# A mixture of experts whose outputs are added to a table in memory instead of being scattered by matmuls

## The chip, the core and the metric

The kernel runs on one core of one Trainium2 chip. The metric is the device time of one execution in microseconds. TensorE is called PE in the profile, VectorE DVE, ScalarE ACT, GpSimd POOL and SyncE SP; PEld is the weight load of a matmul. A trace is one profiled execution, with times in us from the start of its span.

## The reference

Two transformer blocks on 512 tokens of 1024 features. The first has differential attention, then a mixture of experts: 16 experts in 4 groups of 4; a token takes the likeliest group and in it the best two experts. The second block has forgetting attention with pooling, a convolution module and two convolutional feed-forward layers. The change lies in the mixture:

```
gates = one_hot(group) * (g_w * e_w)                     # (512, 16), two per token are not 0
hid = silu(t @ w_gate[e]) * (t @ w_up[e])                # 1024 -> 512, for each expert e
hid = hid * gates[:, e]
y = sum over e of hid @ w_down[e]                        # 512 -> 1024
x = x + g2 * y
```

All data are float32, and all 16 experts' weights (6 MB each) are read.

## The kernel before

The kernel multiplies in a split form: each float32 operand is taken as a high part (float32r, written by ACT) and a low part (the rest, by DVE), and `mm3` (lines 204 to 207) does three matmuls: high by high, high by low, low by high.

Weights come through the class `Weights`. A unit is a load of 1 MB into a raw buffer, issued by SP on the hardware queue; it is split in two halves of 128x1024 (line 106 on ACT for the high part, line 115 on DVE for the low part). In the mixture of experts there are four raw buffers and seven pairs of split buffers (lines 1010 and 1011); up to four units are loaded and six halves split ahead of the matmul that takes them. A raw buffer is free again, and SP issues the next load into it, when both its halves are split.

Features and experts. `moe_constants` (line 834, called near the end of attention) writes the shift of the second modulation, the same for all tokens, into the table `rows` in memory; later the scaled activations of all tokens, `h2tok`, are added to that table by four accumulating DMAs (line 1149). The router then gives each token its place among the tokens of an expert. An expert has 128 slots; `slots` (line 1209) turns them into row numbers (`idi`, and `idf` as a float), where an empty slot has number 600, out of bounds. `gather` (line 1227) clears a buffer on POOL and fetches an expert's rows by an indirect DMA; a row out of bounds is not fetched. Code for experts with more than 128 tokens stands behind a branch (lines 1297 to 1356).

The loop over the 16 experts (line 1453). Iteration e runs on PE in this order:

- `gate_up(e)`: 48 matmuls into two banks; ACT applies Silu, DVE multiplies with the gate and the up part into `sg`
- `x_tiles(e+1)`: eight transposes of the next expert's rows (line 1374), split by ACT and DVE into Xh and Xl
- `prep(e+2)`: four small matmuls that find the rows of the expert after that, and its gather
- `down(e-1)`: 24 matmuls into two banks; `down_evac(e-1)` splits them into Yh and Yl, and DVE writes a one-hot matrix S of slots by tokens (line 1436)
- `hid_t(e)`: four transposes of `sg`, split into Hh and Hl

Experts form groups of 3, 3, 3, 3 and 4 (line 1366). When a group's outputs are there, `scatter` (line 1438) brings them back to the tokens: for each of 8 blocks of 128 features, two matmuls per expert (Yh and Yl against S, lines 1444 and 1445, 512 columns each) add up in a `tp` bank, and DVE adds the bank, times the modulation, to the residual `xT` (line 1446). Four groups are handed out piecewise within the loop, one block per two halves of weights (`take`, line 1380); what is left is done at once two experts later. The last group of four runs after the loop, and each block is followed by `even_prep` (line 1501): the residual is stored, and the next layer's input is written as high (ACT) and low part (DVE).

The layout before: partition p of a weight tile holds rows k*128+p, so a load takes runs of one row: 2 KB for gate and up (512 columns), 4 KB for down (1024 columns).

Of the kernel before, what the change touches and what calls it, by code (L numbers as in the profile page):

```python
# [25 lines left out]
D = 1024  # L26
# [135 lines left out]
def kernel(ctx, tc, a, out):  # L162
# [657 lines left out]
    NONE = 600.0  # L820
    rows = dram.tile([S, D], FT, name="rows")
    gm2 = mk(mcp, (128, KT), FT, "gm2")
    wrg = mk(mcp, (128, KT, 20), FT, "wrg")
# [10 lines left out]
    def moe_constants():  # L834
# [19 lines left out]
        for x in range(2):  # L854
            V.tensor_scalar(first[:, x, :], iota_s[:, 0:4], -3.0 + 2.0 * x, None, op0=OP.add)
        for b in range(2):
            ps = bank("tp")
            for k in range(4):
                T.transpose(ps[:, k * 128:(k + 1) * 128], mod[:, SH2, 4 * b + k:4 * b + k + 1].to_broadcast([128, 128]),
                            ident)  # L860
            sh = mk(at, (128, S), FT, "t", 6)
# [152 lines left out]
    def moe_unit(w, k0, nk, n):  # L1014
        u = k_unit(w, k0, nk, 0, n, (raw_rings, split_rings, cnt[0], cnt[1]))
        cnt[0] += 1
        cnt[1] += 2
        return u
# [190 lines left out]
    def slots(oh, p, bufs=2, n=4):  # L1209
# [7 lines left out]
        V.tensor_scalar(idf, idf, NONE, None, op0=OP.add)  # L1217
        idi = mk(p, (128, 1), I32, "idi", bufs)
        V.tensor_copy(idi, idf)
# [18 lines left out]
    def prep(e, n=52):  # L1238
        idf, idi, i_ps = slots(OH[e], mp, n=n)
        xr = mk(mp, (128, D), FT, "xr", 2)  # L1240
        gather(idi, xr)
        ROWS[e] = (xr, idf)
        if n == 52:
            GC[e] = gate_of(e, mp, i_ps)

    mark(0)
    prep(0, 4)
# [49 lines left out]
    with tc.If(most > 128):  # L1297
        with tc.For_i(0, NE, 1) as ev:
            have = nc.values_load(count[0:1, ds(ev, 1)], min_val=0, max_val=S)
            with tc.If(have > 128):  # L1300
# [5 lines left out]
                for b in range(1, NT):  # L1306
                    idf, idi, i_ps = slots(one_hot(ov, pcol_e[:, :, None], 128 * b, 1), ov, 1, 52)
                    xr = mk(ov, (128, D), FT, "oxr")
                    gather(idi, xr)
                    gall = mk(ov, (128, NE), FT, "ogs")  # L1310
# [11 lines left out]
                    for name, ps in (("expert_w_gate", pg), ("expert_w_up", pu)):  # L1322
                        for q in range(2):
                            w = mk(ov, (128, 4, EF), FT, "ow", 3)
                            nc.sync.dma_start(w, a[name][0, ds(ev, 1), q * 512:(q + 1) * 512, :].rearrange(
                                "o (k p) n -> p (o k) n", p=128))
                            for k in range(4):
# [37 lines left out]
    A.activation(cmax, eps1, AF.Silu)  # L1365
    GROUPS = [(0, 3), (3, 6), (6, 9), (9, 12), (12, 16)]
    def x_tiles(e):
# [9 lines left out]

    spread_out, halves_taken = [iter(())], [0]

    def take(j):  # L1380

        halves_taken[0] += 1
        if halves_taken[0] % 2 == 0:
            next(spread_out[0], None)
        return ws.take(j)

    def gate_up(e):
        hi, lo, gc = XT.pop(e)
        banks = []
        for name in ("g", "u"):  # L1390
            ps = bank("mm")
            banks.append(ps)
            for q in range(2):
                for half in range(2):
                    w = take(U[name, e][q] + half)
                    for kk in range(2):
                        k = 4 * q + 2 * half + kk
                        mm3(ps, (hi[:, k, :], lo[:, k, :]), (w[0][:, kk, :], w[1][:, kk, :]), k == 0, k == KT - 1)
            if name == "g":
                sg = mk(mb, (128, EF), FT, "sg", 2)  # L1400
                A.activation(sg, ps, AF.Silu)
                if e + 2 < NE:
                    mark(e + 2)
        V.scalar_tensor_tensor(sg, sg, gc, banks[1], op0=OP.mult, op1=OP.mult)
        HID[e] = sg

    def hid_t(e):
# [4 lines left out]
        for k in range(4):  # L1412
            T.transpose(ps[:, k * 128:(k + 1) * 128], sg[:, k * 128:(k + 1) * 128], ident)
        split(ps.rearrange("p (a n) -> p a n", n=128), hi, lo)
        HT[e] = (hi, lo)

    def down(e):
        hi, lo = HT.pop(e)
        banks = [bank("sc"), bank("sc")]
        for k in range(4):  # L1420
            w = take(U["d", e][k // 2] + k % 2)
            for half in range(2):
                c = slice(half * 512, (half + 1) * 512)
                mm3(banks[half], (hi[:, k, :], lo[:, k, :]), (w[0][:, 0, c], w[1][:, 0, c]), k == 0, k == 3)
        DB[e] = banks

    def down_evac(e):
        banks = DB.pop(e)
        yh = mk(ysp, (128, D), FR, "Yh", 4)
        yl = mk(ysp, (128, D), FR, "Yl", 4)  # L1430
# [4 lines left out]
        ST[e] = mk(ysp, (128, S), FR, "S", 4)  # L1435
        V.tensor_scalar(ST[e], iota_s, ROWS.pop(e)[1], None, op0=OP.is_equal)

    def scatter(e0, e1, done=None):
        for m in range(KT):
            yield  # L1440
            ps = bank("tp")
            c = slice(m * 128, (m + 1) * 128)
            for e in range(e0, e1):
                T.matmul(ps, lhsT=Y[e][0][:, c], rhs=ST[e], start=e == e0, stop=False)  # L1444
                T.matmul(ps, lhsT=Y[e][1][:, c], rhs=ST[e], start=False, stop=e == e1 - 1)  # L1445
            V.scalar_tensor_tensor(xT[m], ps, mod[:, G2, m:m + 1], xT[m], op0=OP.mult, op1=OP.add)
            if done is not None:
                done(m)

# [3 lines left out]
    for e in range(NE):  # L1453
        if e in [e1 + 2 for _, e1 in GROUPS]:
            for _ in spread_out[0]:
                pass
        gate_up(e)
# [49 lines left out]
    ws.flush(len(ws.halves))  # L1507
    for _ in scatter(*GROUPS[-1], done=even_prep):
        pass
    lows.pop(0)()  # L1510
# [968 lines left out]
```

## Time and profile before

| | us |
|---|---|
| median of 3 runs | 1922.92 |
| lowest, highest | 1920.22, 1924.81 |
| profiled execution | 1918.79 |
| its span | 1917.0 |
| PE busy | 1860.0 |
| DVE busy | 1388.0 |
| ACT busy | 955.0 |

The mean granted clock of PE is 0.982 of full speed. A busy share is an average over stages; the stage in question lies between about 365 and 726 us. A matmul's row shows its full length with its pipeline, about 0.4 us for 512 columns, while the next one starts 0.23 us later: counts of matmuls are therefore priced by distances of starts, not by the length of a row. In the chain of waits a piece is what the end of the execution waited for at that time.

### The profile page before, as it was taken

How to read it: one execution, taken by the hardware profiler on the slowest of the kernel's cores; microseconds unless marked ns; L12 is line 12 of the kernel's file. 1: busy time of each engine (PE TensorE's matmuls, PEld its weight loads, DVE VectorE, ACT ScalarE, POOL GpSimd, SP SyncE). 2: the span in 40 equal slices, each digit the busy share in tenths (PEclk: the TensorE clock that was granted, in tenths of full speed). 3: DMA queues.
4: the chain of work that ended last, by engine and by line, in shares of the span. 5: the costliest groups of instructions: out<-in, count | busy, mean ns of one | idle time of the engine just before them, and what ended most of it. 6: DMA issues, size and time to landing. Idle time of an engine off the chain costs nothing.

```text
span 1917.0 us, 24466 instructions
## 1 busy us (share of the span) xinstructions
PE 1860.0 (97%) x9422; PEld 1524.7 (80%) x9423; DVE 1388.0 (72%) x2431; ACT 955.0 (50%) x1530; POOL 101.9 (5%) x144
## 2 busy tenths in 40 slices
PE   6999999699999999999999999999999999999999
PEld 5787766487888878877888888888778888898898
DVE  6888875699999988677676466367997766647752
ACT  4555554576776665555344244247574644324421
POOL 5000001110100001000000000000000000000000
PEclk9999989799999999999999999999999999999999
DMA  9644326698988872202232232223121222223232
GB/s 284 201 127 137 111 78 211 179 330 305 313 296 283 280 257 78 67 26 85 89 109 88 89 109 88 88 89 88 53 58 45 67 88 88 98 79 110 88 100 78
DMA packets 195947, 260.49 MB, mean 136 GB/s; under 512 B 7489, under 2 KB 144922, under 8 KB 195826
## 3 DMA queue, kind: packets, MB, share of 16 engines
q1 hardware_dynamic: 185378, 228.67, 36.3%
q0 software_dynamic: 10448, 30.20, 5.5%
q8 instruction: 76, 1.25, 0.3%
q14 instruction: 45, 0.37, 0.1%
HBM read 252.56 MB, written 10.49 MB: 137 GB/s over the span
## 4 chain that ended last, share of the span: by engine, by line
PE 86%; DVE 6%; DMA 4%; ACT 2%; issue 1%; SPq 0%; POOL 0%; POOLq 0%; ACTq 0%; DVEq 0%
PE mm L205 11%; PE mm L207 11%; PE mm L206 11%; PE sc L205 10%; PE sc L207 10%; PE sc L206 10%; PE tp L205 1%; PE tp L1444 1%; PE tp L206 1%; PE tp L207 1%; DVE lo L115 1%; PE tp L1445 1%; PE sc L719 1%; DMA ada_q<-in_ada_w_dram 1%; PE sc L2437 1%
## 5 line engine op out<-in xcount | busy, mean ns | idle before, releaser
L106 ACT ACTIVATE hi<-raw 128x1024 fp32r<-128x1024 f32 (+1 forms) x409 | 414.8, 1040 | 205.4 <-PE sc L2439 39.9
L115 DVE TENSOR_TENSOR lo<-raw,hi 128x1024 fp32r<-128x1024 f32 (+1 forms) x409 | 481.7, 1202 | 23.6 <-ACT hi L106 22.1
L205 PE MATMUL mm<-h,hi 128*128 128x512 f32 x592 | 242.3, 409 | 2.7 <-DVE vl L153 1.9
L206 PE MATMUL mm<-h,hi 128*128 128x512 f32 x592 | 234.6, 396 | 1.3 <-DVE h L153 1.3
L207 PE MATMUL mm<-h,lo 128*128 128x512 f32 x592 | 234.7, 396 | 0.0
L205 PE MATMUL sc<-h,hi 128*128 128x512 f32 x552 | 219.4, 397 | 0.0
L207 PE MATMUL sc<-h,lo 128*128 128x512 f32 x552 | 217.8, 395 | 0.2 <-DVE lo L115 0.2
L206 PE MATMUL sc<-h,hi 128*128 128x512 f32 x552 | 217.2, 394 | 0.0
L2045 ACT ACTIVATE y<-u,VC 128x512 f32<-128x512 f32 x88 | 71.7, 817 | 161.2 <-DVE u L153 161.1
L205 PEld LDWEIGHTS mm<-h,hi 128*128 128x128 f32 x592 | 112.6, 190 | 30.9 <-issue 7.0
L153 DVE SCALAR_TENSOR_TENSOR y<-u,VC,y 128x511 f32<-128x511 f32 (+1 forms) x176 | 131.5, 748 | 3.4 <-ACT y L2045 0.2
L207 PEld LDWEIGHTS mm<-h,lo 128*128 128x128 f32 x592 | 112.2, 190 | 25.7
L206 PEld LDWEIGHTS mm<-h,hi 128*128 128x128 f32 x592 | 112.7, 190 | 24.6 <-DVE h L153 2.4
L207 PEld LDWEIGHTS sc<-h,lo 128*128 128x128 f32 x552 | 104.0, 188 | 24.7 <-DVE lo L115 0.9
L205 PEld LDWEIGHTS sc<-h,hi 128*128 128x128 f32 x552 | 104.2, 189 | 23.4 <-issue 0.9
L206 PEld LDWEIGHTS sc<-h,hi 128*128 128x128 f32 x552 | 104.2, 189 | 23.0
L205 PE MATMUL mm<-hi,Xh 128*128 128x512 f32 x256 | 103.4, 404 | 0.0
L206 PE MATMUL mm<-lo,Xh 128*128 128x512 f32 x256 | 102.1, 399 | 0.0
L207 PE MATMUL mm<-hi,Xl 128*128 128x512 f32 x256 | 102.0, 398 | 0.0
L153 DVE TENSOR_TENSOR u<-sc,rb 128x512 f32<-128x512 f32 x51 | 35.2, 691 | 85.1 <-PE sc L207 81.3
L153 DVE TENSOR_TENSOR u<-mm,rb 128x512 f32<-128x512 f32 x37 | 25.5, 691 | 66.7 <-PE mm L207 62.8
L2055 ACT ACTIVATE act<-y 128x512 fp32r<-128x512 f32 x44 | 27.8, 632 | 82.6 <-DVE y L153 82.6
(567 smaller groups left out, 3991.7 us busy)
## 6 DMA issues: line engine op xcount, KB each, us to landing
raw<-in_ffn_w_up_dram SPq DMA_DIRECT2D x44, 1024.0 KB, 5.1
raw<-in_expert_w_gate_dram SPq DMA_DIRECT2D x32, 1024.0 KB, 6.9
raw<-in_expert_w_up_dram SPq DMA_DIRECT2D x32, 1024.0 KB, 7.6
raw<-in_expert_w_down_dram SPq DMA_DIRECT2D x32, 1024.0 KB, 7.1
ada_w<-in_ada_w_dram POOLq DMA_DIRECT2D x32, 512.0 KB, 4.0
raw<-in_ffn_w_down_dram SPq DMA_DIRECT2D x16, 1024.0 KB, 5.2
ada_q<-in_ada_w_dram SPq DMA_DIRECT2D x32, 256.0 KB, 6.8
raw<-in_odd_w_pw_dram SPq DMA_DIRECT2D x16, 512.0 KB, 4.2
```

The lines of the kernel that those rows point to most:

```text
L106: nc.scalar.activation(hv, src, AF.Copy)
L115: self.nc.vector.tensor_tensor(lv, src, hv.bitcast(FT), op=OP.subtract)
L153: r = f(*x, **kw)
L205: T.matmul(ps, lhsT=l[0], rhs=r[0], start=start, stop=False)
L206: T.matmul(ps, lhsT=l[0], rhs=r[1], start=False, stop=False)
L207: T.matmul(ps, lhsT=l[1], rhs=r[0], start=False, stop=stop)
L719: T.matmul(ps[s], lhsT=q[x][r, c], rhs=kx[y][r, :], start=n3 == 0, stop=n3 == 2)
L1444: T.matmul(ps, lhsT=Y[e][0][:, c], rhs=ST[e], start=e == e0, stop=False)
L1445: T.matmul(ps, lhsT=Y[e][1][:, c], rhs=ST[e], start=False, stop=e == e1 - 1)
L2045: A.activation(y, u, AF.Identity, scale=wcol(2), bias=col("ffn_b", l * 2 * FT_N + ch))
L2055: A.activation(hi, y, AF.Copy)
L2437: T.matmul(p, lhsT=l_[0], rhs=wv[1][:, kk, :], start=False, stop=False, skip_group_check=True)
```

## The change

- Experts 0 to 13: ACT copies the two banks of `down` into one float32 tile Y, and an indirect DMA on POOL adds its rows to a table `ysum` in memory (512 tokens by 1024 features); empty slots are out of bounds and are skipped. `ysum` is cleared by eight DMAs in `moe_constants`.
- Experts 14 and 15 keep Yh, Yl and S. After the scatter-add of expert 13, `table` loads `ysum` back in two DMAs of 1 MB. After the loop, for each of the 8 feature blocks, four transposes put the table into a bank (`summed`), and the matmuls of experts 14 and 15 (`placed`) add to it. For the first four blocks the table and expert 14 come before expert 15's output is awaited. The groups, `scatter` and the piecewise hand-out go.
- `hid_t(15)` runs in the middle of `down(14)`.
- Weights: partition p now holds whole rows, p*8 to p*8+7 for gate and up, p*4 to p*4+3 for down, so a load takes runs of 8 KB. The features are therefore kept in another order: `h2tok` and the shift in `rows` are written with a step of 128 floats, and gate and up are read from PSUM with a step of four floats when `sg` is written.
- The gather's buffers are cleared once, before the loop, and no more before each gather.

```diff
-    def k_unit(w, k0, nk, c0, n, rings=None):
-        src = w[k0 * 128:(k0 + nk) * 128, c0:c0 + n].rearrange("(k p) n -> p k n", p=128)
+    def k_unit(w, k0, nk, c0, n, rings=None, whole=False):
+        if whole:
+            src = w.rearrange("(p k) n -> p k n", p=128)[:, k0:k0 + nk, c0:c0 + n]
+        else:
+            src = w[k0 * 128:(k0 + nk) * 128, c0:c0 + n].rearrange("(k p) n -> p k n", p=128)
...
+        zero = mk(at, (128, S), FT, "t", 6)
+        V.memset(zero, 0.0)
+        for t in range(NT):
+            for b in range(2):
+                nc.sync.dma_start(ysum[t * 128:(t + 1) * 128, b * 512:(b + 1) * 512], zero)
+        sh = [mk(at, (128, S), FT, "t", 6) for _ in range(2)]
         for b in range(2):
...
-            A.activation(sh, ps, AF.Copy)
-            for t in range(NT):
-                nc.sync.dma_start(rows[t * 128:(t + 1) * 128, b * 512:(b + 1) * 512], sh)
+            for x in range(2):
+                A.activation(sh[x].rearrange("p (k a) -> p a k", k=4)[:, 64 * b:64 * b + 64, :],
+                             ps.rearrange("p (a k) -> p a k", k=8)[:, :, 4 * x:4 * x + 4], AF.Copy)
+        for t in range(NT):
+            for x in range(2):
+                nc.sync.dma_start(rows[t * 128:(t + 1) * 128, x * 512:(x + 1) * 512], sh[x])
...
-        A.activation(h2tok[:, :, m * 128:(m + 1) * 128], ps, AF.Copy)
+        A.activation(h2tok.rearrange("p t (k a) -> p t a k", k=8)[:, :, 16 * m:16 * m + 16, :],
+                     ps.rearrange("p t (a k) -> p t a k", k=8), AF.Copy)
...
     def gather(idi, xr):
-        G.memset(xr, 0.0)
...
+    xrs = [mk(mp, (128, D), FT, "xr", 2) for _ in range(2)]
+    for xr in xrs:
+        G.memset(xr, 0.0)
...
-                sg = mk(mb, (128, EF), FT, "sg", 2)
-                A.activation(sg, ps, AF.Silu)
+                sg = mk(mb, (128, 4, 128), FT, "sg", 2)
+                A.activation(sg, ps.rearrange("t (p k) -> t k p", k=4), AF.Silu)
...
-        V.scalar_tensor_tensor(sg, sg, gc, banks[1], op0=OP.mult, op1=OP.mult)
+        V.scalar_tensor_tensor(sg, sg, gc, banks[1].rearrange("t (p k) -> t k p", k=4), op0=OP.mult, op1=OP.mult)
...
-    def down(e):
+    def down(e, middle=None):
...
+            if k == 2 and middle is not None:
+                middle()
...
+    LATE = NE - 2
     def down_evac(e):
         banks = DB.pop(e)
+        if e < LATE:
+            y = mk(ysp, (128, D), FT, "Y", 2)
+            for half in range(2):
+                A.activation(y[:, half * 512:(half + 1) * 512], banks[half], AF.Copy)
+            nc.gpsimd.indirect_dma_start(out=ysum, out_offset=bass.IndirectOffsetOnAxis(ap=ROWS.pop(e)[2][:, :1], axis=0),
+                                         in_=y, in_offset=None, bounds_check=S - 1, oob_is_err=False, compute_op=OP.add)
+            return
...
+    def table():
+        for x in range(2):
+            ysums.append(mk(ysp, (128, NT, D // 2), FT, "yt", 2))
+            nc.gpsimd.dma_start(ysums[x], ysum[:, x * 512:(x + 1) * 512].rearrange("(t p) n -> p t n", p=128))
+    def summed(m, ps):
+        for t in range(NT):
+            T.matmul(ps[:, t * 128:(t + 1) * 128], lhsT=ysums[m // 4][:, t, m % 4 * 128:(m % 4 + 1) * 128], rhs=ident,
+                     is_transpose=True, start=t == 0, stop=False, skip_group_check=True)
+    def placed(e, m, ps):
+        for x in range(2):
+            T.matmul(ps, lhsT=Y[e][x][:, m * 128:(m + 1) * 128], rhs=ST[e], start=False,
+                     stop=e == NE - 1 and x == 1, skip_group_check=True)
...
         if e:
-            down(e - 1)
-            if e < NE - 1:
-                down_evac(e - 1)
-        hid_t(e)
-        if e == NE - 1:
+            down(e - 1, middle=None if e < NE - 1 else lambda: hid_t(NE - 1))
             down_evac(e - 1)
-        for e0, e1 in GROUPS:
-            if e1 == e:
-                spread_out[0] = scatter(e0, e1)
+        if e == LATE:
+            table()
+        if e < NE - 1:
+            hid_t(e)
...
-    for _ in scatter(*GROUPS[-1], done=even_prep):
-        pass
+    sums_ps = {}
+    for m in range(4):
+        sums_ps[m] = bank("mm" if m % 2 else "tp")
+        summed(m, sums_ps[m])
+        placed(LATE, m, sums_ps[m])
+    for m in range(KT):
+        if m not in sums_ps:
+            sums_ps[m] = bank("mm" if m % 2 else "tp")
+            summed(m, sums_ps[m])
+            placed(LATE, m, sums_ps[m])
+        placed(NE - 1, m, sums_ps[m])
+        V.scalar_tensor_tensor(xT[m], sums_ps[m], mod[:, G2, m:m + 1], xT[m], op0=OP.mult, op1=OP.add)
+        even_prep(m)
```

## Rows read from the trace of the kernel before

**Rows 1.** The page, part 1: engine, busy us, share of the span, instructions.

```profile
PE 1860.0 (97%) x9422; PEld 1524.7 (80%) x9423; DVE 1388.0 (72%) x2431; ACT 955.0 (50%) x1530; POOL 101.9 (5%) x144
```

**Rows 2.** Windows: us; PE, PEld, DVE, ACT, POOL busy (instructions); clock, DMA share, GB/s.

```profile
400.00:420.00 20.00, 20.00 (x97) 16.31 (x96) 19.33 (x26) 15.32 (x21) 2.28 (x2) 1.00 0.97 343
```

**Rows 3.** Chain of waits, 392 to 740 us: start us, us, what.

```profile
411.02 0.87 PE tp L1374 x8
...
429.31 0.87 PE tp L1374 x8
...
451.79 0.87 PE tp L1374 x8
...
477.76 0.87 PE tp L1374 x8
...
496.05 0.87 PE tp L1374 x8
...
677.14 0.87 PE tp L1374 x8
```

**Rows 4.** Line 1444: operation, count, ns min/median/max, first to last start us.

```profile
L1444 PE MATMUL tp<-S,Yh x128: 387/392/500, 440.4 to 723.3; 128*128 128x512 f32 x128
```

**Rows 5.** Timeline of DVE, 392 to 452 us: start, us, operation [idle before].

```profile
395.06 0.15 DVE L153 TENSOR_REDUCE idf<-sm 128x1 f32<-128x4 f32 x1
...
400.11 1.28 DVE L153 TENSOR_TENSOR Yl<-sc,Yh 128x512 fp32r<-128x512 f32 x2
401.31 0.48 DVE L153 TENSOR_SCALAR S<-iota_s,idf 128x512 fp32r<-128x512 f32 x1
...
413.32 1.29 DVE L153 TENSOR_TENSOR Xl<-tp,Xh 128x512 fp32r<-128x512 f32 x2 [0.60 <-ACT Xh L198]
414.53 0.15 DVE L153 TENSOR_REDUCE idf<-sm 128x1 f32<-128x4 f32 x1
```

**Rows 6.** DMA, 400 to 440 us, one value per us; queues: packets, MB, share.

```profile
GB/s 379 393 426 401 414 236 143 381 397 152 252 377 401 401 389 305 346 395 303 371 389 393 340 397 365 111 262 399 334 150 313 395 360 373 391 330 373 383 357 381
...
q1 hardware_dynamic: 5431, 12.99, 91.7%
q0 software_dynamic: 365, 0.64, 4.7%
```

**Rows 7.** DMA queue of POOL, 343 to 355 us (the accumulates of line 1149).

```profile
q0 software_dynamic: 548, 2.04, 94.8%
```

**Rows 8.** DMA issues of the page: count, KB each, median us to landing.

```profile
rows<-h2tok POOLq DMA_DIRECT2D x4, 512.0 KB, 9.0
```

**Rows 9.** Two reductions of `before` (lines 1179, 1181): ns min/median/max, start us.

```profile
L153 DVE TENSOR_REDUCE ahead<-before x1: 420/420/420, 343.7 to 343.7; 128x64 f32<-128x256 f32 x1
...
L153 DVE TENSOR_REDUCE back<-before x1: 592/592/592, 344.1 to 344.1; 128x64 f32<-128x256 f32 x1
```

**Rows 10.** Timeline from the last `down` to the next stage, PE and DVE.

```profile
702.72 0.51 PE L205 MATMUL sc<-hi,Hh 128*128 128x512 f32 x1 [1.41 <-DVE Hl L153]
...
710.47 0.47 PE L1444 MATMUL tp<-S,Yh 128*128 128x512 f32 x1 [0.51 <-DVE gfe L153]
...
711.45 0.74 DVE L153 SCALAR_TENSOR_TENSOR xT<-tp,mod,xT 128x512 f32<-128x512 f32 x1
...
723.74 0.39 PE L205 MATMUL mm<-h,hi 128*128 128x512 f32 x1
...
724.60 1.63 DVE L153 SCALAR_TENSOR_TENSOR h<-xT,gfe,h 128x512 fp32r<-128x512 f32 x2
```

**Rows 11.** Timeline of SP, 276 to 292 us; then one piece of the chain.

```profile
280.07 6.36 SPq L864 DMA_DIRECT2D rows<-t  x8
286.54 0.92 SPq L79 DMA_DIRECT2D raw<-in_attn_w_out_dram  x1
...
323.52 0.24 PE sc L205
```

More of the change, by code (lines that the diff above doesn't have):

```diff
@@ L821 @@
     rows = dram.tile([S, D], FT, name="rows")
+    ysum = dram.tile([S, D], FT, name="ysum")
     gm2 = mk(mcp, (128, KT), FT, "gm2")
@@ L1014, in moe_unit @@
     def moe_unit(w, k0, nk, n):
-        u = k_unit(w, k0, nk, 0, n, (raw_rings, split_rings, cnt[0], cnt[1]))
+        u = k_unit(w, k0, nk, 0, n, (raw_rings, split_rings, cnt[0], cnt[1]), whole=True)
         cnt[0] += 1
@@ L1217, in slots @@
         V.tensor_scalar(idf, idf, NONE, None, op0=OP.add)
-        idi = mk(p, (128, 1), I32, "idi", bufs)
+        idi = mk(p, (128, 1), I32, "idi", 2 * bufs)
         V.tensor_copy(idi, idf)
@@ L1239, in prep @@
         idf, idi, i_ps = slots(OH[e], mp, n=n)
-        xr = mk(mp, (128, D), FT, "xr", 2)
-        gather(idi, xr)
-        ROWS[e] = (xr, idf)
+        gather(idi, xrs[e % 2])
+        ROWS[e] = (xrs[e % 2], idf, idi)
         if n == 52:
             GC[e] = gate_of(e, mp, i_ps)
+    xrs = [mk(mp, (128, D), FT, "xr", 2) for _ in range(2)]
+    for xr in xrs:
+        G.memset(xr, 0.0)
     mark(0)
@@ L1308 @@
                     xr = mk(ov, (128, D), FT, "oxr")
+                    G.memset(xr, 0.0)
                     gather(idi, xr)
@@ L1324 @@
                             w = mk(ov, (128, 4, EF), FT, "ow", 3)
-                            nc.sync.dma_start(w, a[name][0, ds(ev, 1), q * 512:(q + 1) * 512, :].rearrange(
-                                "o (k p) n -> p (o k) n", p=128))
+                            nc.sync.dma_start(w, a[name][0, ds(ev, 1), :, :].rearrange(
+                                "o (p k) n -> p (o k) n", p=128)[:, 4 * q:4 * q + 4, :])
                             for k in range(4):
@@ L1365 @@
     A.activation(cmax, eps1, AF.Silu)
-    GROUPS = [(0, 3), (3, 6), (6, 9), (9, 12), (12, 16)]
     def x_tiles(e):
@@ L1376, in x_tiles @@
         XT[e] = (hi, lo, GC.pop(e))
[L1378 to L1385, printed above, removed]
     def gate_up(e):
@@ L1394, in gate_up @@
                 for half in range(2):
-                    w = take(U[name, e][q] + half)
+                    w = ws.take(U[name, e][q] + half)
                     for kk in range(2):
@@ L1412, in hid_t @@
         for k in range(4):
-            T.transpose(ps[:, k * 128:(k + 1) * 128], sg[:, k * 128:(k + 1) * 128], ident)
+            T.transpose(ps[:, k * 128:(k + 1) * 128], sg[:, k, :], ident)
         split(ps.rearrange("p (a n) -> p a n", n=128), hi, lo)
         HT[e] = (hi, lo)
-    def down(e):
+    def down(e, middle=None):
         hi, lo = HT.pop(e)
@@ L1420, in down @@
         for k in range(4):
-            w = take(U["d", e][k // 2] + k % 2)
+            if k == 2 and middle is not None:
+                middle()
+            w = ws.take(U["d", e][k // 2] + k % 2)
             for half in range(2):
@@ L1425, in down @@
         DB[e] = banks
+    LATE = NE - 2
     def down_evac(e):
         banks = DB.pop(e)
-        yh = mk(ysp, (128, D), FR, "Yh", 4)
-        yl = mk(ysp, (128, D), FR, "Yl", 4)
+        if e < LATE:
[5 more added lines that the diff above has]
+            return
+        yh = mk(ysp, (128, D), FR, "Yh", 2)
+        yl = mk(ysp, (128, D), FR, "Yl", 2)
         for half in range(2):
@@ L1434, in down_evac @@
         Y[e] = (yh, yl)
-        ST[e] = mk(ysp, (128, S), FR, "S", 4)
+        ST[e] = mk(ysp, (128, S), FR, "S", 2)
         V.tensor_scalar(ST[e], iota_s, ROWS.pop(e)[1], None, op0=OP.is_equal)
[L1438 to L1448, printed above, removed]
+    ysums = []
+    def table():
[10 more added lines that the diff above has]
+                     stop=e == NE - 1 and x == 1, skip_group_check=True)
     ws.load_ahead, ws.split_ahead = 4, 6
@@ L1453 @@
     for e in range(NE):
-        if e in [e1 + 2 for _, e1 in GROUPS]:
-            for _ in spread_out[0]:
-                pass
         gate_up(e)
@@ L1507 @@
     ws.flush(len(ws.halves))
-    for _ in scatter(*GROUPS[-1], done=even_prep):
-        pass
+    sums_ps = {}
[11 more added lines that the diff above has]
+        even_prep(m)
     lows.pop(0)()
```

1 line of the change is left out of this document (removed).

## The prediction

> **What bounds the kernel now.** I read the page first: TensorE (PE) is busy for 97% of the span [rows 1], so removed matmuls count unless another engine stands right behind. The change touches the mixture of experts, about 365 to 726 us, so everything else is read there. The windows come next. In 400 to 420 us PE is busy for all 20.00 us, VectorE (DVE) for 19.33, the DMA engines for 0.97, at the full clock of 2.4 GHz (1.00) [rows 2]: three limits lie within a few per cent of each other.
>
> The chain of waits separates them. Each expert leaves one mark there, the eight transposes of line 1374. With no scatter in between, marks lie 18.29 us apart (411.02 to 429.31, and 477.76 to 496.05). With a group's scatter they lie 22.48 (to 451.79) and 25.97 us (to 477.76) apart [rows 3]. Three experts thus take 66.74 us where three bare ones would take 54.87, and the 11.87 us are the group's 48 matmuls of lines 1444 and 1445 (0.247 each, small stalls included). From 411.02 to 677.14 are twelve experts and four groups, 266.12 us; all 128 uses of line 1444 lie between 440.4 and 723.3 us [rows 4].
>
> The timeline of DVE shows what stands behind PE. In the scatter-free stretch one cycle of DVE, from one idf reduction to the next, takes 414.53 - 395.06 = 19.47 us, longer than PE's 18.29, with 0.60 us idle [rows 5]. There DVE fell behind and PE lived on weight halves split in advance; the scatters gave DVE time to catch up. If PE's scatters alone went, the loop would run at DVE's 19.47. What the change takes from DVE therefore matters as much as what it takes from PE.
>
> **The change part by part.**
>
> *Scatter out of the loop.* For 14 experts the matmuls, their one-hot S, the low halves Yl and (for all in-loop groups) the xT updates go. PE's floor over the twelve experts is 12 x 18.29 = 219.5 instead of 266.12: **-46.6 us**.
>
> DVE's cycle loses two Yl (1.28) and one S (0.48) [rows 5]: 19.47 - 1.76 = 17.7, now 0.6 below PE. ACT keeps two evacuations of the same size (plain copies), and is busy 15.32 of 20 us [rows 2]. PE paces the loop, narrowly.
>
> *DMA.* An expert reads 6 x 1 MB = 6.29 MB of weights. In 400 to 440 us the hardware queue moved 12.99 MB in 91.7% of 40 us, so 6.29 MB cost 17.8 us; two gathers moved 0.64 MB in 4.7%, 0.94 us each [rows 6]. A scatter-add moves the same rows, 0.32 MB. The only accumulating DMA in the trace took 94.8% of 12 us for 2.04 MB [rows 7]: 5.6 us per MB, so 1.8 us. The sum is 20.5 us per expert, above PE's 18.29. But the share also counts packets that wait as the queue restarts: the same row of GB/s falls to 143, 152, 111 and 150 just four times, and runs near 390 between, up to 426 [rows 6]. At 390 the weights take 16.1, the sum 18.9; at 426, 14.8 and 17.5. Whole rows make runs of 8 KB out of 2 KB (gate, up) and 4 KB (down). No row shows an 8 KB run; its gain lies between nothing (18.9) and the best slice (17.5). I take a value near the middle, just under PE's pace, and charge 0.25 us per expert for DMA and DVE so close behind: **+3.0 us** over twelve (0 to 12 x (20.5 - 18.29) = 26.5).
>
> The queues: on POOL the scatter-add of e-1 waits for ACT's copies and for the previous scatter-add, and the next gather stands behind it. One expert lies between the two, and a 0.5 MB accumulate landed in 9.0 us [rows 8], so that gather is in time. POOL loses the memset of each gather and gains a DMA issue, inside its 2.28 busy us of 20 [rows 2]. Y has two buffers, reused two experts later.
>
> *Strided reads.* Gate and up are now read from PSUM with a step of four floats (16 bytes). The one such pair in the trace is two reductions of the same 256 numbers: 420 ns in order, 592 ns at that step [rows 9], 0.67 ns per element. For 512 that is +0.34 us on DVE's sg, and at most as much on ACT's Silu. DVE comes to 18.1, still under 18.29: nothing. The Trainium skill, "Advanced Engine Details and Errata", section Memory Cachelines, says that full speed wants accesses that stay in one line of 16 bytes (SBUF) or 8 bytes (PSUM), and that crossing each time is penalised; these rows agree for SBUF, and no run here shows it for PSUM. By the rule alone DVE could set the pace, which is rival B; the rows keep it under PE.
>
> *Table and tail.* Two 1 MB reads of the table share the DMA with expert 15's weights: 2.1 MB are 5.4 us at 390 GB/s, and its own weights are in flight by then: **+0.8** (0 to 5.4).
>
> hid_t(15) moves into the middle of down(14). It removed a wait of 1.41 us [rows 10] at most, but down(15) next waits for down(14)'s banks to be evacuated: **-0.5** (0 to 1.4).
>
> The last group: once Y15 is there (710.47), PE now runs 58 matmuls, to 723.74, 0.229 each [rows 10]. Afterwards the table's transposes and expert 14's matmuls of the first four blocks run while Y15 is evacuated. What is left is 8 matmuls for these, and per later block 4 transposes (0.11 each, eight take 0.87 [rows 3]) and 4 matmuls: 1.8 + 4 x 1.36 = 7.2 us, 6.1 less. But DVE has 16 operations of about 0.75 (xT and h) from 711.45; back to back they end 13.0 after 710.47, where they now end 15.8 after (726.23) [rows 10]: 2.8 less. The next stage needs both. I take the middle, **-4.4**.
>
> *Before the loop.* Eight more table writes stand on SP's queue ahead of the last attn_w_out load: eight took 6.36 us, so that load starts at 292.9 instead of 286.54 [rows 11]. Its block starts at 323.52 [rows 11]; even with 9.0 us to land [rows 8] it has 21 us. A memset of 128x512, two extra ACT copies and strided writes of h2tok lie partly on the chain: **+0.5** (0 to 2).
>
> The path for more than 128 tokens per expert changes too; gathers move 0.32 MB, 78 rows, so it stays unused.
>
> Sum: -46.6 + 3.0 + 0.8 - 0.5 - 4.4 + 0.5 = -47.2 us. The profiled execution took 1918.79 (span 1917.0), so 1871.6; the median before, 1922.92, lies 4.1 higher, and I give the time for that: **1875.7 us**. Its own range, from no drag and the full tail (-53) to half of the DMA bound (-34), is 1870 to 1889.
>
> **The rivals.**
>
> *A. DMA becomes the bound (0.22).* Eight-kilobyte runs bring nothing, and the accumulates interleave with the weights: 20.5 us per expert. For: the share of 0.97 [rows 2]. Against: 426 GB/s at times [rows 6]. Loop 12 x 20.5 = 246, 20.1 less instead of 46.6; with the other terms -23.7: 1899. The Trainium skill, "DMA: Bandwidth & Descriptors", section Specifications, gives about 358 GB/s as a core's share of HBM, by which 6.9 MB would take an estimated 19.4 us; the slices up to 426 GB/s contradict it as a ceiling for a core alone.
>
> *B. DVE sets the pace (0.08).* It serves its queue in order; if strided PSUM reads cost three times the 0.34, and its idle time rises from 0.60 to 1, the cycle is 17.7 + 1.0 + 0.4 = 19.1. Loop +9.8 against PE's floor: 1882.
>
> *C. Slower: the accumulates hold the engines (0.06).* Place: the 14 scatter-adds. If reading, adding and writing scattered rows keeps the weights out for the whole 9.0 us that an accumulate takes to land [rows 8], an expert costs 17.8 + 0.9 + 9.0 = 27.7, 12 x 27.7 = 332, 66 more than now: about 1985. It decides from 22.5 us per expert on, an accumulate of 3.8 us, twice what I worked out.
>
> *D. The runs stay cut (0.04).* If the queue cuts the 8 KB runs into packets as before, and only that goes wrong, the loop sits at the 18.9 of 390 GB/s: -46.6 + 7.3 - 3.6 = -43: 1880.
>
> **How the numbers follow.** My forecast has 0.60, A 0.22, B 0.08, C 0.06, D 0.04. The range for 8 in 10 leaves out C and the far half of A: 1867 to 1897. A measurement here tells 0.2% (3.8 us) from no change. All but C are faster: A's worst end (20.5 with the table's 5.4 as well) is still 19 us under before. I leave 0.02 for no change and 0.07 for slower.
>
> **What would show it.** Right: the marks of line 1374 stay 18.3 to 18.6 us apart from the third expert on; no matmul reads S before the end; DVE idles more than 0.6 us a cycle; the hardware queue has about 28,700 fewer packets (64 x 384 for gate and up, 32 x 128 for down); the last scatter takes 7 to 8 us on PE. Wrong: marks of 19 us or more; with ACT waiting for raw it is A, with DVE back to back it is B; a software queue share far over 10% in the loop is C.

## The result, and the profile after

| | us |
|---|---|
| before, median of 4 runs | 1921.57 |
| after, median of 4 runs | 1896.24 (1895.38 to 1896.68) |
| ratio after / before | 0.9875, 95% interval 0.9862 to 0.9888 |
| forecast | 1875.7, range 1867 to 1897 |

The change gains 25.3 us, where 47.2 were forecast. Rival A (1899) lies nearer than the forecast.

From span start to end, the two profiled executions differ by 22.3 us (1917.0 and 1894.7). The marks split that: front to the first mark -1.1, marks 0 to 3 -0.2, the twelve experts from mark 3 to mark 15 **-28.0**, from mark 15 to the last `h` of the next stage **+7.7**, all the rest -0.7. So the loop gained less than forecast (-46.6 + 3.0 = -43.6), and the tail lost where it should have gained.

The page of after, part 1, answering [rows 1]:

```profile
PE 1815.7 (96%) x9230; PEld 1484.7 (78%) x9231; DVE 1346.3 (71%) x2358; ACT 955.8 (50%) x1532; POOL 117.2 (6%) x146
```

PE lost 44.3 us of busy time, close to the 46.6 forecast for the loop, yet the span lost 22.3: the rest has become idle time. The marks of the expert loop (now line 1392; timeline of PE: start, us, operation), answering [rows 3]:

```profile
409.51 1.03 PE L1392 MATMUL tp<-ident,xr 128*128 128x128 f32 x8
427.79 1.03 PE L1392 MATMUL tp<-ident,xr 128*128 128x128 f32 x8
446.05 1.03 PE L1392 MATMUL tp<-ident,xr 128*128 128x128 f32 x8
465.88 1.03 PE L1392 MATMUL tp<-ident,xr 128*128 128x128 f32 x8
488.05 1.03 PE L1392 MATMUL tp<-ident,xr 128*128 128x128 f32 x8
...
647.59 1.04 PE L1392 MATMUL tp<-ident,xr 128*128 128x128 f32 x8
```

Two intervals keep PE's floor (18.28 and 18.26), then come 19.83 and 22.17 and, but for one more of 18.28, 19.1 to 21.9: 238.08 us for the twelve, 19.84 each, where before had 266.12. The windows show when PE runs dry, answering [rows 2]:

```profile
400.00:420.00 20.00, 20.00 (x97) 16.30 (x96) 18.45 (x23) 16.27 (x21) 4.02 (x3) 1.00 0.98 360
420.00:600.00 180.00, 170.20 (x803) 136.85 (x802) 156.51 (x190) 132.67 (x163) 30.18 (x18) 0.99 0.95 341
```

In 420 to 600 us PE is idle for 9.8 us, and DVE for 23.5, so neither is busy all the time. Who waits for whom (engine, line, releaser: us, times, longest):

```profile
ACT hi L106 <- DMA raw<-in_expert_w_down_dram: 24.7, 15, 2.9
DVE lo L115 <- ACT hi L106: 13.0, 13, 2.3
...
ACT hi L106 <- DMA raw<-in_expert_w_gate_dram: 9.8, 7, 2.1
PE mm L206 <- DVE lo L115: 9.3, 7, 2.1
```

It reads from the bottom: PE waits for a low half, DVE for the high half, ACT for a load. The chain of waits of one round (start us, us, what) closes the ring:

```profile
421.06 8.74 DMA raw<-in_expert_w_gate_dram
...
429.91 1.06 ACT hi L106
430.97 0.49 ACT Xh L198
...
431.48 1.29 DVE Xl L153 x2
...
433.29 4.54 DVE lo L115 x4
...
439.48 1.23 DVE lo L115
...
440.72 9.41 DMA raw<-in_expert_w_gate_dram
```

A load lands in 8.7 us; ACT and DVE, each in order, come through its half, the next expert's rows and five low halves before a raw buffer is free again; the next load on the chain starts 19.66 us after the first, about one interval of the marks. The DMA queues in 400 to 600 us (packets, MB, share; then issues, KB, median us to landing), answering [rows 6, 8]:

```profile
q1 hardware_dynamic: 8668, 63.12, 83.5%
q0 software_dynamic: 2880, 5.27, 11.3%
...
raw<-in_expert_w_gate_dram SPq DMA_DIRECT2D x20, 1024.0 KB, 8.7
...
ysum<-Y,idi POOLq DMA_INDIRECT x11, 11.2
xr<-rows,idi POOLq DMA_INDIRECT x10, 5.1
```

The same stretch of before:

```profile
q0 software_dynamic: 1390, 2.43, 4.0%
...
raw<-in_expert_w_gate_dram SPq DMA_DIRECT2D x18, 1024.0 KB, 6.9
```

The gate loads landed in 6.9 us there and in 8.7 now; the software queue's share was 4.0% and is 11.3%. In the tail, from the last `down` to the next stage, answering [rows 10] (first ACT, then PE):

```profile
679.23 1.06 ACT L106 ACTIVATE hi<-raw 128x1024 fp32r<-128x1024 f32 x1 [4.64 <-DMA raw<-in_even_w_in_dram]
```

```profile
681.55 0.80 PE L205 MATMUL sc<-hi,Hh 128*128 128x512 f32 x1 [6.16 <-DVE Yl L153]
682.15 0.63 PE L206 MATMUL sc<-lo,Hh 128*128 128x512 f32 x1
682.57 0.63 PE L207 MATMUL sc<-hi,Hl 128*128 128x512 f32 x1
...
692.82 0.40 PE L1475 MATMUL tp<-S,Yh 128*128 128x512 f32 x1
...
700.55 0.47 PE L205 MATMUL mm<-h,hi 128*128 128x512 f32 x1 [0.24 <-DVE xT L153]
```

`down(15)` waits 6.16 us for the evacuation of expert 14, which stands on ACT behind a half of the next stage whose load is late. After that pause PE runs at the lower of its two levels (1.2 GHz) for a while: starts lie 0.42 us apart instead of 0.23. The granted clock of the 20 us is 0.81, 0.63 in the first ten and 1.00 in the rest:

```profile
680.00:700.00 20.00, 18.45 (x85) 15.00 (x85) 12.19 (x19) 7.08 (x11) 2.37 (x5) 0.81 0.44 138
```

`down(15)` takes 7.7 us (681.55 to 689.22), 5.7 before. The last group itself (692.82 to 700.55) takes 7.7 us, as forecast.

### The profile page after: what moved, and what is told of

It reads as the page before. It is cut to its first block, busy times and chain, and to the rows that moved or that the text cites. A ratio compares the mean times of both kernels' runs of the same rounds, so it can differ in the third digit from the quotient of the medians.

```text
span 1894.7 us, 24058 instructions
## 1 busy us (share of the span) xinstructions
PE 1815.7 (96%) x9230; PEld 1484.7 (78%) x9231; DVE 1346.3 (71%) x2358; ACT 955.8 (50%) x1532; POOL 117.2 (6%) x146
## 3 DMA queue, kind: packets, MB, share of 16 engines
q1 hardware_dynamic: 157858, 230.77, 35.9%
## 4 chain that ended last, share of the span: by engine, by line
PE 72%; DVE 11%; DMA 11%; ACT 4%; issue 2%; SPq 0%; POOL 0%; ACTq 0%; POOLq 0%; DVEq 0%
PE sc L205 9%; PE sc L207 9%; PE sc L206 9%; PE mm L205 8%; PE mm L207 8%; PE mm L206 8%; DVE lo L115 5%; DMA raw<-in_expert_w_gate_dram 4%; DMA ada_q<-in_ada_w_dram 1%; PE tp L205 1%; PE tp L206 1%; PE tp L207 1%; PE sc L722 1%; ACT hi L106 1%; PE sc L2470 1%
## 5 line engine op out<-in xcount | busy, mean ns | idle before, releaser
L206 PEld LDWEIGHTS mm<-lo,Xh 128*128 128x128 f32 x256 | 49.1, 192 | 27.2 <-DVE lo L115 15.9
```

Of the source, the lines that this page charges most:

```text
L206: T.matmul(ps, lhsT=l[0], rhs=r[1], start=False, stop=False)
```

## The experiments

All stages are measured inside the traces, because the stages around the loop, whose code is nearly or wholly the same in the kernels of the table, vary: the front up to the first mark took 363.5 to 368.8 us, the part behind the last `h` 1191.4 to 1198.0. The table holds the ratio to before with its interval, the mean interval of the marks from 3 to 15, and the tail from mark 15 to the last `h`. "Tail lead 5" splits five halves ahead, in place of six, from the last expert on. "The same" is five raw buffers with tail lead 5. The light kernels of experiment 5 had one execution each; only their traces are used.

| kernel | ratio (95%) | us per expert | tail us |
|---|---|---|---|
| before | 1 | 22.18 | 47.6 |
| after | 0.9875 (0.9862 to 0.9888) | 19.84 | 55.4 |
| after, again | 0.9870 (0.9849 to 0.9892) | 19.56 | 54.7 |
| no adds | 0.9793 (0.9777 to 0.9810) | 18.27 | 50.8 |
| plain writes | 0.9844 (0.9816 to 0.9872) | 19.15 | 53.7 |
| five raw buffers | 0.9811 (0.9795 to 0.9827) | 18.69 | 51.4 |
| cut rows | 0.9922 (0.9905 to 0.9938) | 20.13 | 56.8 |
| before with whole rows | 1.0005 (0.9994 to 1.0017) | 22.16 | 47.7 |
| tail lead 5 | 0.9851 (0.9834 to 0.9869) | 19.54 | 48.8 |
| no table read | 0.9867 (0.9838 to 0.9897) | 19.42 | 50.4 |
| five raw + tail lead 5 | 0.9790 (0.9777 to 0.9804) | 18.66 | 48.7 |
| the same, two adds | 1.0256 (1.0232 to 1.0281) | 25.9 (437 to 670 us) | 59.7 |
| the same, no gather | 0.9763 (0.9747 to 0.9778) | 18.27 | 44.6 |
| the same, free banks | 0.9804 (0.9785 to 0.9823) | 18.65 | 47.2 |
| six raw, six split | 0.9803 (0.9786 to 0.9819) | 18.78 | 46.0 |

**1. No adds.** Theory 1: the added row traffic starves the weight ring. Rival 2: the loads alone do.

```diff
-            nc.gpsimd.indirect_dma_start(out=ysum, out_offset=..., in_=y, ..., compute_op=OP.add)
+            ROWS.pop(e)
             return
```

> The fourteen accumulating scatters into the table are left out (the evacuations into Y by ScalarE stay, the experts 0 to 13 are missing from the output). Everything else is the changed kernel: 8 KB weight rows, gathers, table reads. Theory 1, the accumulates take DMA time from the weight loads and stretch them: from the fourth mark on the interval falls from 19.84 us to the matmul floor of 18.3 to 18.6, 238.1 us of loop become 220 to 223, and the whole run is 1875 to 1881 (-15 to -21 against the changed kernel's 1896.2). Rival 2, the loop is held by the weight loads alone (their 8 KB rows, or the four raw buffers): the interval stays at 19.5 to 19.9 and the run within 3 us of 1896. If both have a share, the interval lands between, and its fall gives the accumulates' part.

The windows of that kernel, 420 to 600 us:

```profile
420.00:600.00 180.00, 180.00 (x868) 146.89 (x867) 170.31 (x208) 146.54 (x178) 12.06 (x10) 1.00 0.96 360
```

Every interval is 18.24 to 18.31 us and PE has no idle time, with the same 8 KB rows and four raw buffers. Rival 2 is out. The DMA share is 0.96, as in after (0.95): the share doesn't tell a sufficient DMA from an insufficient one.

**2. Plain writes.**

```diff
-                                         in_=y, ..., oob_is_err=False, compute_op=OP.add)
+                                         in_=y, ..., oob_is_err=False)
```

> The changed kernel with the fourteen scatters written plainly instead of added (the table then holds each token's last expert alone). Same rows, same queue, same place. Theory 1, split in two: without the scatters the interval was 18.27 us, with them 19.84. If the price is the adding (a second pass over the row at the table), a plain write gives most of it back: interval 18.3 to 18.7, run 1877 to 1883. If the price is the row packets themselves and their place between the weight rows, half or more stays: interval 19.0 to 19.8, run 1886 to 1895.

19.15 us, against 19.56 and 19.84 with the adding and 18.27 without scatters: the larger part of the price stays. By the run's time the two can't be told apart (the intervals overlap).

**3. Five raw buffers**, the other way to mend a starved ring.

```diff
-    raw_rings = [(raw_pool, 2), (mw, 2)]
+    raw_rings = [(raw_pool, 2), (mw, 3)]
...
-    ws.load_ahead, ws.split_ahead = 4, 6
+    ws.load_ahead, ws.split_ahead = 5, 6
```

> The changed kernel with five raw weight buffers in place of four, loads issued five units ahead in place of four; to make room sg has one buffer in place of two and the squares ahead of the expert loop one in place of three (worth under 1 us in front, to be read from the first mark, 363.5 before). Theory 1a, the ring closes on latency: a load of some 9 us, ScalarE's hi, VectorE's lo and the release add up to 19.8 us for a ring of four; with a fifth buffer the loads lie a unit further ahead and the interval falls to 18.3 to 18.8, the run to 1879 to 1886. Rival 2a, the DMA engines' throughput (343 GB/s, busy 0.93 to 0.99) is the limit: a fifth buffer only makes each load wait longer on its queue (landing 10 to 12 us in place of 9), the interval stays at 19.5 to 19.9 and the run at 1893 to 1897.

Both theories are half right. Its marks:

```profile
524.21 1.04 PE L1392 MATMUL tp<-ident,xr 128*128 128x128 f32 x8
542.60 1.03 PE L1392 MATMUL tp<-ident,xr 128*128 128x128 f32 x8
562.38 1.03 PE L1392 MATMUL tp<-ident,xr 128*128 128x128 f32 x8
581.47 1.03 PE L1392 MATMUL tp<-ident,xr 128*128 128x128 f32 x8
600.69 1.03 PE L1392 MATMUL tp<-ident,xr 128*128 128x128 f32 x8
```

The floor holds up to 542.60, then the intervals are 19.78, 19.09, 19.22. The extra buffer covers the shortfall for more experts, and shows what the loop comes to when the reserve is gone: 19.0 to 19.3 us with five (last five intervals, three traces), 19.5 to 20.2 with four (last seven, four traces).

**4. No gather, two adds** (both on five raw buffers with the tail's shorter lead). To tell whether the 19.1 us with five buffers are a matter of bytes:

```diff
-        gather(idi, xrs[e % 2])
+        if e < 2:
+            gather(idi, xrs[e % 2])
```

> Same base, the gathers of experts 2 to 15 left out (their rows are those of experts 0 and 1), the adds kept. Theory, bytes: 6.56 MB an expert need 18.2 us at 360 GB/s, so TensorE's 18.27 us is the interval throughout, loop 219 to 220 us, run 1873 to 1878. Rival, the adds are special (they read and write the table, 328 us per thousand packets of 4 KB against 159 for a gather's): the gather is cheap and its absence gives back less than half of the 0.78 us: interval at the end 18.7 us or more, run within 3 us of 1880.

```profile
420.00:600.00 180.00, 180.00 (x868) 146.82 (x867) 171.52 (x209) 146.05 (x177) 13.95 (x9) 1.00 0.99 360
```

The floor throughout (18.24 to 18.31), with all adds in place: with five buffers the adds alone don't hold the loop. Leaving out either half of the row traffic gave the floor, the adds with four buffers, the gathers with five; no gathers with four was not run. Since PE's floor is the limit in both, how the price divides between gather and add is not shown.

```diff
-            nc.gpsimd.indirect_dma_start(out=ysum, ..., in_=y, ..., compute_op=OP.add)
+            idi = ROWS.pop(e)[2]
+            for _ in range(2):
+                nc.gpsimd.indirect_dma_start(out=ysum, ..., in_=y, ..., compute_op=OP.add)
```

> Base: the kernel with five raw buffers and the shorter split lead in the tail (1880.5 us, 0.979 of before; its interval 18.3 us in the first eight and 19.05 at the end, at 360 GB/s). Here every scatter is issued twice (the table holds each sum twice). Theory, bytes: the DMA engines move no more than about 360 GB/s in this loop; 6.29 MB of weights, 0.27 of gather and 0.27 of scatter make 6.83 MB or 19.0 us, a second scatter 7.11 MB or 19.7 to 19.8 us, from an earlier expert on; loop of twelve 232 to 237 us in place of 223.9, run 1888 to 1893. Rival, latency: the ring's round trip is what closes the loop, the second add lands behind the first on its own queue and only spreads the same load: interval 19.0 to 19.2, run within 3 us of 1880.

A miss for both: 25 to 27 us an expert, slower than before (22.18), while the DMA engines moved only 275 GB/s (420 to 600 us). Its waits:

```profile
POOL ysum L1448 <- DMA ysum<-Y,idi: 61.9, 7, 9.8
DVE idi L153 <- DMA ysum<-Y,idi: 58.9, 7, 8.9
...
PE mm L206 <- DVE lo L115: 37.2, 7, 6.3
```

The second add waits for the first to land (11.2 us), and DVE's next write of the index tile waits for both; behind it in DVE's queue stand the low halves that PE needs. This experiment says nothing on bytes. It shows another limit close by: one add fits beside the gather, two don't. With one add that limit doesn't act: among the waits of after in 400 to 600 us there is none of DVE for the index tile, and none of POOL for an add to land.

**5. The DMAs by themselves.** Two of three matmuls and the low halves are left out, so that only the loads, rows and ACT can hold the loop.

```diff
-                        mm3(ps, (hi[:, k, :], lo[:, k, :]), (w[0][:, kk, :], w[1][:, kk, :]), k == 0, k == KT - 1)
+                        T.matmul(ps, lhsT=hi[:, k, :], rhs=w[0][:, kk, :], start=k == 0, stop=k == KT - 1)
...
```

> Base: five raw buffers and the shorter split lead. Of each of the experts' three matmuls only the first (high by high) is left, and VectorE's low halves of their weights are left out, so that TensorE and VectorE need some 6 and 11 us an expert and ScalarE some 15; all loads, gathers and adds stay. The interval is then the DMA engines' own. Theory, a ceiling near 360 GB/s: 6.83 MB an expert take 19.0 us, the interval that the base reached at the end of its loop (19.05). Rival, the DMA engines could go faster and the base is held by the ring's hand-over between load, ScalarE and VectorE: 15 to 17.5 us, 390 GB/s or more.

> As the light kernel, and the gathers of experts 2 to 15 and the adds left out too: weights alone, 6.29 MB an expert. Theory, a ceiling near 360 GB/s: 17.5 us, and the difference to the light kernel (1.5 us) is the price of the rows of one expert. Rival: 15 to 16.2 us (390 to 420 GB/s, or ScalarE), and the rows cost what is left to the light kernel's interval.

> The light kernel with its weight rows cut as before (2 KB for gate and up, 4 KB for down), gathers and adds kept: what the 8 KB rows are worth when the DMA engines alone set the pace. Theory (the changed kernel with cut rows was 0.3 to 0.7 us an expert slower): 19.4 to 20.0 us against the light kernel's. Rivals: the same interval within 0.1 us (runs of 2 KB cost nothing); or 20.5 and more, which is what the shares of the kernel before added up to.

Windows of the light kernel, then of the one without rows:

```profile
420.00:560.00 140.00, 98.87 (x307) 59.37 (x306) 27.70 (x65) 108.86 (x135) 18.38 (x14) 0.68 0.99 367
```

```profile
420.00:560.00 140.00, 104.59 (x368) 62.09 (x368) 34.52 (x85) 135.22 (x169) 0.00 (x0) 0.83 1.01 421
```

The intervals are 18.53 with rows, 14.93 without, 19.30 with rows and cut runs. In the light kernel no compute engine is busy for over 78%, and in most rounds PE waits for the gathered rows:

```profile
514.91 1.94 PE L1395 MATMUL tp<-ident,xr 128*128 128x128 f32 x8 [1.31 <-DMA xr<-rows,idi]
```

So 18.53 is an upper bound for the DMAs, not their exact need; and 14.93 is one too, since ACT is busy for 135 of 140 us there. Weights alone flow at 421 GB/s; the rows of one expert, about 0.5 MB, add 3.6 us to this loop. Cutting the runs to 2 and 4 KB adds 0.8. An estimate of how full the DMAs were with rows: loads land after 12.0 to 13.0 us there and one is issued every 3.09 us (18.53 / 6), so on average about four of the five raw buffers have a load under way. That speaks for 18.53 being near the need of weights and rows together, without showing it.

The Trainium skill ("DMA: Bandwidth & Descriptors", Specifications) gives about 358 GB/s as a core's share of HBM; the row of 421 GB/s over 140 us lies above it, so it was no ceiling here, where one core runs alone.

**6. Row length in the real loop.** Cut rows in after, and whole rows in before (the hidden columns, the table and `h2tok` in the matching order each time):

```diff
-        u = k_unit(w, k0, nk, 0, n, (raw_rings, split_rings, cnt[0], cnt[1]), whole=True)
+        u = k_unit(w, k0, nk, 0, n, (raw_rings, split_rings, cnt[0], cnt[1]))
...
```

> The changed kernel with the weight rows cut as in the kernel before (runs of 2 KB for gate and up, 4 KB for down; hidden columns, table and h2tok in the old order), everything else of the change kept: table, accumulates, skipped slots, tail. Theory 3, the long runs are what slows the loads: interval under 19.4, run 1883 to 1890, landing times back to 7 us. Theory 1, the accumulates and the DMA engines' total time are what limits: short runs take as long or longer, interval 19.8 to 21, run 1896 to 1912.

> The kernel before with the change's long rows alone (8 KB per partition for gate, up and down, hidden columns, table of rows and h2tok in the matching order); the scatter by TensorE stays. Theory: the kernel before is paced by TensorE (busy 312 of 313 us of loop), so faster loads give nothing: 22.2 us an interval, 1915 to 1922. Rival, the loads had a hidden share in its pace (clock dips, waits that the busy count covers): 1900 to 1912.

After with cut rows is slower by 0.5% of before, 0.3 to 0.6 us an expert. In before, whole rows change nothing (1.0005): PE was busy for 179.30 of 180 us there too. Eight-kilobyte rows are worth something only where the DMAs have become tight.

**7. The tail.** The half that stands ahead of the evacuation, and the table reads that delay its load:

```diff
+        if e == NE - 1:
+            ws.split_ahead = 5
         if e:
             down(e - 1, middle=...)
```

> The changed kernel, but from the last expert's down onwards the weight stream splits five halves ahead in place of six, so that the half of the next stage, whose load landed late (12.8 us), is no longer ahead of the evacuation of expert 14 on ScalarE. Theory: that head-of-line wait (4.6 us on ScalarE, 6.2 us on TensorE, then half clock) is what turned the tail's gain into a loss; without it the last mark to the next stage falls from 53.0 to 44 to 47 us and the run to 1887 to 1890. Rival: the tail is held by the table's 2 MB and the last loads on the DMA engines, and the wait moves to the next half or to the table read: the tail stays over 50 us, the run within 2 us of 1896.

```diff
-            nc.gpsimd.dma_start(ysums[x], ysum[:, x * 512:(x + 1) * 512].rearrange("(t p) n -> p t n", p=128))
+            G.memset(ysums[x], 0.0)
```

> The changed kernel with the two table reads (2 MB) left out and the tiles set to zero by GpSimd (the output lacks experts 0 to 13); the accumulates stay. Theory: the reads fall into the tail's most crowded 12 us, stretch the loads of the next stage to 12.8 us and so cause the head-of-line wait of 4.6 us: without them last mark to last h falls from 55.4 us to 48 to 51, the run by 4 to 7 us, to 1889 to 1892, the loop unchanged at 19.8. Rival, that load is late because the weight ring runs late by itself: tail 53 us or more, run within 2 us of the change's.

The first matmul of `down(15)` in the two, with its wait (6.16 us in after):

```profile
677.00 0.50 PE L205 MATMUL sc<-hi,Hh 128*128 128x512 f32 x1 [1.89 <-DVE Yl L153]
```

```profile
676.18 0.74 PE L205 MATMUL sc<-hi,Hh 128*128 128x512 f32 x1 [1.90 <-DVE Yl L153]
```

Both shorten the tail: from 55.4 to 48.8 us without the head-of-line wait, to 50.4 without the reads. The long wait needs both: a late load, and a place ahead of the evacuation. (With the shorter lead ACT still waits 5.82 us for that load, but now behind the evacuation.) The time of the kernel without the reads does not show it (0.9867): in its trace the part behind the last `h` came out 6.3 us longer than in after's, with the same code.

**8. Towards a better version.** Five raw buffers and the shorter lead together; then the last `down` in banks that are already free; then six raw buffers against one pair of split buffers.

> The fifth raw buffer and the shorter split lead in the tail together. The fifth buffer alone measured 0.9811 of the kernel before, the tail alone 0.9851, the change 0.9875. If the two are independent: 0.9787, some 1877 us on this chip, with an interval of 18.7 us and last mark to the last h of 47 to 49 us. If the tail's wait is one of the DMA engines that the fifth buffer already covers in part: 0.980 to 0.981.

```diff
-        banks = [bank("sc"), bank("sc")]
+        tag = "mm" if e == NE - 1 else "sc"
+        banks = [bank(tag), bank(tag)]
...
```

> Same base, a candidate for a best version: the last expert's down writes the two banks that gate and up have left, in place of the two that still wait for expert 14's evacuation, and the sums of the table use the freed ones. Theory: the wait of 1.9 us of TensorE for Yl in the tail goes, and with it the stretch at 0.87 of the clock: last mark to last h 45 to 47 us in place of 48.7, run 1.5 to 3.5 us under the base, 0.977 to 0.978 of before. Rival: the stream of halves for that down is late by itself (VectorE's lo), the wait turns into one for lo and nothing changes: 0.979.

> A second candidate: six raw buffers, loads six units ahead; the room comes from the ring of split halves (six in place of seven, split five ahead in place of six), the rest as with five raw buffers and the shorter split lead (0.979 of before, 18.3 us for eight experts, then 19.05). The light kernel gave 18.53 us an expert for the DMA engines alone. Theory: a deeper ring keeps them busy all the time, the interval holds 18.3 us for some twelve experts and then goes to 18.6; loop of twelve 219.5 to 221 us in place of 223.9, run 2 to 4 us less, 0.977 to 0.978. Rival: the shorter ring of halves lets ScalarE's and VectorE's queues reach TensorE: interval 18.8 us or more from the start, 0.980 to 0.985.

The first two steps add up as expected: 0.9790, 0.9% under after. The wait in the tail that the free banks were to remove is gone in the trace (47.2 for 48.7), but the ratio (0.9804) is no better. Six raw buffers keep the floor for seven of the twelve intervals, with single ones of 19.5 to 20.3 us between, where ACT waits for loads and DVE for ACT: 0.9803. Neither is an improvement that can be measured. The best version is five raw buffers with the shorter lead; its interval overlaps that of five raw buffers alone (0.9811), and it is the tail in the traces (48.7 for 51.4) that tells the two apart.

**9. After, again.**

> The changed kernel itself, once more: its loop took 238.1, 234.5 and 233.0 us in three traces with the same loop (its own, the one with the shorter split lead, the one without table reads). Expected: 233 to 238 us again, a time of 0.9875 of before within 0.2%, and so a second trace of its tail (55 us from the last mark to the last h if that wait belongs to the code, under 51 if it was one execution's).

234.7 us of loop and a tail of 54.7, with 5.78 us of wait at the same place: both losses belong to the code. The loop of after ranges over 233.0 to 238.1 in the four traces that share it.

## Why the prediction was wrong, step by step

The profiled executions differ by 22.3 us where 47.2 were forecast. Of the missing 24.9 us, 15.6 lie in the loop (-28.0 for -43.6) and 11.8 in the tail (+7.7 for -4.1); the front and the rest came out 2.5 better than forecast.

- *Scatter out of the loop, PE's floor at 18.29.* Right: 18.24 to 18.31 in every interval wherever the row traffic was about halved. DVE was idle for 23.5 of 180 us, so it doesn't pace the loop.
- ***The charge for DMA and DVE close behind, +3.0 us.*** This step failed. It measured 12 x (19.56 to 19.84 - 18.29) = 15.2 to 18.6 us. Two errors are in it. First, the DMA sum was taken just under PE's pace, from between 17.5 and 18.9. The weights were priced well (14.8 at 426 GB/s, at most 14.93 measured), but the rows of an expert, taken at 0.94 + 1.8 = 2.7 us, added 3.6 to the light loop; so the sum may lie as high as 18.5, above PE's 18.29. Second, a tie was charged 0.25 us an expert, when over the twelve it costs 1.3 to 1.55 with four raw buffers; with five it costs nothing for some eight experts and 0.7 to 1.0 after that. The reading that fits, though no run shows it by itself, is that the weights fall behind whenever rows are under way, and that a ring of four has no reserve to make that up. That the floor returns with no adds on four buffers, with no gathers on five, and for eight experts with a fifth buffer alone shows both parts, the rows and the depth. How the 19.1 us of the five-buffer ring divide between the DMAs' need and the hand-over stays open: the light kernel bounds the first at 18.53.
- *Strided reads, nothing.* Right, and cheaper than the bound from [rows 9]: DVE's `sg` and ACT's Silu, in order in before and with the step in after (400 to 600 us of both traces; shape, count, busy us, mean ns of one, idle):

```profile
L153 DVE SCALAR_TENSOR_TENSOR sg<-sg,gc,mm 128x512 f32<-128x512 f32 x9 | 6.7, 743 | 1.0 <-PE mm L207 1.0
L1401 ACT ACTIVATE sg<-mm 128x512 f32<-128x512 f32 x9 | 5.3, 589 | 5.3 <-PE mm L207 5.3
```

```profile
L153 DVE SCALAR_TENSOR_TENSOR sg<-sg,gc,mm 128x512 f32<-128x512 f32 x10 | 7.4, 741 | 0.1
L1410 ACT ACTIVATE sg<-mm 128x512 f32<-128x512 f32 x10 | 5.8, 580 | 0.7 <-PE mm L207 0.7
```

  743 and 741 ns, 589 and 580. DVE is busy for about 17.3 us an expert (170.31 of 180 us in the kernel without adds); the forecast cycle was 18.1 with 0.6 idle in it. The Trainium skill ("Advanced Engine Details and Errata", Memory Cachelines) would have a penalty here; these rows show none for PSUM at a step of 16 bytes.
- *Table reads +0.8 and `hid_t(15)` -0.5.* Wrong. From mark 15 to the end of `down(15)` it is 41.6 us (647.59 to 689.22), where before had 31.4: +10.2. This is the second step that failed. The reads cost near their bound of 5.4 (the tail is 4.4 to 5.0 us shorter without them), but by a way that the sum didn't have: a late load, a half on ACT that waits for it 4.64 us, the evacuation behind it, 6.16 us on PE, and then the lower clock level, by which `down(15)` takes 2.0 us longer. `hid_t(15)` in the middle of `down(14)` kept waits of 0.88 and 0.69 us.
- *The last group, -4.4.* Right: from the end of `down(15)` to the next stage's first matmul 11.3 us, 15.3 before, -4.0. Up to the last `h`, where the split above ends, it is 13.7 and 16.2, -2.5: DVE ends later than PE, as the prediction had it.
- *Before the loop, +0.5.* Not to be told: it came out 1.3 shorter (front and marks 0 to 3), while the front of the kernels in the table varies by 5.3.
- *Packets, 28,700 fewer.* The hardware queue has 27,520 fewer (185378 and 157858). Of the 1,150 between, the eight DMAs that clear the table are 1,024 if each of their 128 rows is a packet. Rival D is out.
- *The rivals.* A came nearest in time and in its sign (ACT waiting for raw), but its 20.5 us and its reason were not it: 8 KB rows do bring 0.8 us in the light kernel, and weights and rows together need at most 18.53. That its 1899 lies so near is in part luck: its loop of 246 us is 8 too long, and it had the tail gain where it lost. B is out. C does not happen with one add; with two the loop is slower than before, by the queue and the index tile (275 GB/s), not by the DMA engines' time.

## What to carry to other kernels

Where a removed bottleneck leaves a second resource within some per cent of the first, price the tie by the depth of the buffers between them: leave out or halve the second's traffic, and add one buffer, before trusting the floor. A busy share of the DMA engines is no measure of their need (0.95 in the loop that was held, 0.96 in one that was not): run the loop with the compute thinned out. At the end of a loop, look at what an in-order engine has queued ahead of the evacuation that everything waits for.

## What the runs showed of the hardware that was not expected

Indirect DMAs of rows are dear beyond their bytes: 0.5 MB of rows added 3.6 us to a loop whose weights alone move at 421 GB/s (at that rate 0.5 MB would be an estimated 1.2 us). An add of some 0.25 MB lands after 11.2 us, a plain write of the same rows after 9.8. In the kernel with two adds the index tile was held until the add had landed, and DVE, which writes the next one, waited for that 58.9 of 180 us. A stage with unchanged code, the part behind the last `h`, took 1191.4 to 1198.0 us in the kernels of the table, 6.6 us apart.
